# A host-side second layout of x for the pre-norm, and GpSimd powers for the inverse roots

## The chip, the cores and the metric

The kernel runs on one core of one Trainium2 chip. The metric is the device time of one launch in microseconds, the median of several runs. All other times here come from one profiled execution of the kernel before, whose trace lists every instruction of the five engines (TensorE, VectorE, ScalarE, GpSimd and SyncE, which issues the DMAs; in the profile PE, DVE, ACT, POOL and SP) and every DMA.

## What is computed

One layer of a hybrid decoder, 4096 tokens of 1024 channels, batch 1:

```python
shift, scale, gate = jnp.split(c_act @ ada_w + ada_b, 3, axis=-1)
h = _rmsnorm(x, g_pre) * (1.0 + scale[:, None]) + shift[:, None]
proj = h @ w_in                      # heads of three mixers and their gates
attn = _sliding_window_attention(aq, ak, av, sinks) * jax.nn.silu(ag)
rwkv = _rwkv7_mixer(h, rr, rk, rv, ...) * jax.nn.silu(rg)
gla = _gla_mixer(h, gq, gkk, gv, ...) * jax.nn.silu(gg)
y = jnp.concatenate([attn, rwkv, gla], axis=-1) @ w_out
return x + gate[:, None] * _rmsnorm(y, g_post)
```

Four places need an inverse root: the RMS norm of `x` (one number per token), the norm of the GLA output (per token and head), the group norm of the RWKV output (per position and head) and the RMS norm of `y` (per token). All products of h are done as three float16 products of high and low halves.

## The kernel before

**Two phases.** The tokens go in 16 blocks of 256. A first phase makes h of every block, writes it to memory (`hscr`) and runs the RWKV and GLA mixers, whose states pass from block to block. The second phase reads h back, does the attention, the gates, the output projection (seven products by a scheme of sums of halves) and the final norm. Ahead of the first block stands a prologue, which loads 8 MB of `ada_w` and works out the shift and scale columns `sh` and `gs` that the modulated norm needs.

**Streams and a planner.** Each phase is written as generators (`stage_a`, `stage_p`, `stage_q2`, ...), one per part and block. `emit` interleaves them; `Order` notes every instruction and `pin` then simulates the whole phase with a table of costs per instruction and fixes the order of the instructions on each engine. At run time each engine (and the SP queue, through which all the DMAs of this part go) works strictly in that order: an instruction that waits holds up everything behind it on its engine. Since all calls pass through one helper (`Lane`), almost every row of the profile has the line L334; rows are told apart by their tiles.

**Making h: `stage_a` (L1013).** For block i it loads 256 tokens into `xt`, with tokens on partitions (two groups of 128 tokens, 1024 channels each; one buffer), squares both groups on ScalarE with a running sum (`ssx`), turns the sums into inverse roots `rsx` on VectorE, scales both groups by them, and then needs channels on partitions. That takes 16 transposes of 128x128 on TensorE into a PSUM bank (tag `tr`, tile `tp`), four at a time; ScalarE moves each quarter out with scale and shift (`hf`), rounds it to float16 (`hT`), and VectorE takes the difference as the low half. `stage_p` (L1053) then multiplies `hT` with the weights (`pv`, `lp`, `zz`, `gqk`).

**Inverse roots.** `rsqrt(y, v, n)` (L428) makes `v**-0.5` for n columns on VectorE: a shift and an integer subtraction from the constant `magic`, then three Newton steps of three instructions, 11 dependent instructions in all. It is called in `stage_a` (`rsx`, n = 2), `gla_norm` (`orr`, n = 8), `stage_q2` (`yr`, n = 8) and `norm` in the second phase (`ry`, n = 1, twice per block). The last block's two groups use `last_norm` (L1878), which writes a similar sequence out (`ln`, nine instructions from the sum to the factor).

Of the kernel before, what the change touches and what calls it, by code (L numbers as in the profile page):

```python
# [63 lines left out]
class Order:  # L64
# [34 lines left out]
    def note(self, eng, name, outs, ins, func, r):  # L99
# [9 lines left out]
        if e == "PE":  # L109
            f32, lhs = ins[0].dtype == F32, self.region(ins[0])  # L110
            n = math.prod(o.shape[1:])
            _, p0, p1, _ = self.region(o)
            rows, cs = (lhs[1] // 32, (lhs[2] + 31) // 32), (p0 // 32, (p1 + 31) // 32)
            rows, cs = [(0, 4) if b - a > 2 else (a, b) for a, b in (rows, cs)]
            mode = (rows[1] - rows[0], cs[1] - cs[0])
            took = n * (2 if f32 else 1) / 2400 + 0.003
            took = max(took, 0.056 if not f32 else 0.0 if mode[1] < 4 else 0.109 if n > 16 else 0.21)
            issue = 0.017 if f32 and mode == (1, 2) else 0.009 if f32 and mode[0] == 1 else 0.007
            cells = [4 * a + b for a in range(*rows) for b in range(*cs)]
            st.array = (mode, cells, 2 if f32 and name == "matmul" else 1, took, issue)  # L120
            st.occ = st.lat = 0.0
        elif e == "SP":
            st.bytes = math.prod(ins[0].shape) * SIZE[ins[0].dtype]
            kb = st.bytes / 1024
            st.occ = 0.47
            st.lat = next((t for k, t in ((8, 1.9), (32, 2.0), (128, 2.3), (256, 2.6), (512, 3.5)) if kb <= k), 4.8)
        elif e == "Activation":
            st.occ = (0.05 if on_psum else 0.093) + 0.093 * (len(ins) - 1) + 0.832e-3 * n
            st.lat = st.occ + 0.1
            if len(outs) > 1:  # L130
                st.occ += 0.187
                st.lat = st.occ + 0.02
# [263 lines left out]


@with_exitstack
def hybrid_kernel(ctx, tc, x, rows, ada1, adaw, w1, wl, w2, wo, cst, abias, out):
    nc = tc.nc  # L400
    model = Model(tc)
    V = Lane(model, nc.vector, *LANES[0])
# [19 lines left out]
        a, b = VC[name]  # L422
        return vt[:, a:b] if j is None else vt[:, a + j : a + j + 1]

    magic = cp.tile([P, 16], I32, name="magic")
    V.memset(magic, 0x5F3759DF)

    def rsqrt(y, v, n):  # L428
        ii = st.tile([P, 16], I32, tag="nwi", name="nwi")
        tt = st.tile([P, 16], F32, tag="nwt", name="nwt")  # L430
# [213 lines left out]
    with ExitStack() as p1:  # L644

        soon = ("tables", "scolb", "uw", "w0p0", "w0p1", "one16", "mu_s", "mu_c", "a0h")
        late = ("td", "tf0", "tf1", "Sst0", "Sst1", "lnx")
        tags = ("gvh", "gvl", "hf", "b1", "gl", "bl", "cs", "ch", "gw", "zs", "gaw", "gacc", "zl0", "zl1", "zl2", "early",
                "zb1", "ta", "em", "ep", "zb0", "b2", "zb2", "kg", "kt", "egm", "egp", "qg", "vg", "c2", "middle",
                "AS", "osb", "c3", "KB", "ATm", "c1", "RA", "UV", "BK", "cd", "em0", "bon", "ysb", "rs", "Ss", "lasts")  # L650
        wk1 = {n: pool_of(p1, f"work1{n}", 1) for n in tags}
# [52 lines left out]
                SP.dma_start(t, cst[:, at : at + t.shape[-1]])  # L704
                at += t.shape[-1]

        def load_x(i):
            xt = t_x()
            SP.dma_start(xt, x[i * NT : (i + 1) * NT, :].rearrange("(a p) d -> p a d", p=P))
            E[i]["xt"] = xt  # L710


        scolb = pp.tile([P, KD, 32], F32, name="scolb")
# [299 lines left out]
        def stage_a(i):  # L1013

            yield [("a", i - 1), ("p", i - 2)]
            e = E[i]
            if i > 0:
                load_x(i)
            xt = e["xt"]
            yield [xt, "tr"]  # L1020
            xs = [xt[:, a, :] for a in range(2)]
            jx = wt([P, 2, NT], "hf", 2).rearrange("p a n -> p (a n)").bitcast(F16)
# [12 lines left out]
            e["hT"] = hT  # L1035
            for kp in range(KD // 2):

                tag = "tr" if i else ("tr", "y", "sq", "tr")[kp]
                tp = pst(tag, "tp").rearrange("p (a n) -> p a n", a=2)
# [4 lines left out]
                hf = wt([P, 2, NT], "hf", 2)  # L1044
                for kk in range(2):
                    k = 2 * kp + kk
                    S.activation(hf[:, kk, :], tp[:, kk, :], AF.Identity, scale=gs[:, k : k + 1], bias=sh[:, k : k + 1])
                S.activation(hT[:, 0, 2 * kp : 2 * kp + 2, :], hf, AF.Identity)
                V.tensor_sub(hT[:, 1, 2 * kp : 2 * kp + 2, :], hf, hT[:, 0, 2 * kp : 2 * kp + 2, :])
                yield [hf, "tr"] if i else None  # L1050
            SP.dma_start(hscr[i], hT.rearrange("p a k t -> p (a k t)"))

        def stage_p(i):  # L1053
# [823 lines left out]

    def last_norm(f, h, sums, xt):  # L1878

        v, y, t = [st.tile([P, 1], F32, tag=f"ln{n}", name=f"ln{n}") for n in range(3)]  # L1880
# [302 lines left out]
def _layout(inp):  # L2183
# [14 lines left out]
    def blk(w):  # L2198
# [25 lines left out]
    arrs = [("x", g["x"][0]), ("rows", rows), ("ada1", ada1), ("adaw", adaw), ("w1", w1), ("wl", wl), ("w2", w2),  # L2224
            ("wo", wob), ("cst", cst), ("abias", abt)]
    return {"in_" + n: np.ascontiguousarray(a) for n, a in arrs}

# [13 lines left out]
```

## Time and profile before

| | |
|---|---|
| median of 3 runs | 2062.37 us (2061.8 to 2066.6) |
| profiled execution, span of its instructions | 2056.7 us (the page has no other time of that execution) |
| instructions | 61151 |
| ScalarE busy | 1130.8 us (55%) |
| GpSimd busy | 220.5 us (11%) |
| DMA, mean over the span | 118 GB/s, 35.6% of the 16 engines on the main queue |
| first phase | the first block's values (`pv`) start at 40.1 us, the last inverse root of an RWKV output (`yr`) is done at 1072.3 us |
| second phase | from there to the end |

A row of a group of instructions reads: line, engine, operation, output<-inputs by the program's names, shapes, count, then busy time and mean length of one, then the idle time of the engine ahead of them and who ended it. TensorE's records overlap, because one matrix product is issued before the one ahead has ended: what a product costs the stream of TensorE is the distance from its start to the next start, not its length.

### The profile page before, as it was taken

The numbers are of one execution on the slowest core, as the hardware profiler recorded it, in microseconds if no ns is written. First come the engines' busy times: TensorE is split into PE (matmuls) and PEld (weight loads), VectorE is DVE, ScalarE is ACT, GpSimd is POOL, SyncE is SP. The second block draws the span as 40 slices with busy tenths as digits, with TensorE's granted clock in tenths as the row PEclk, the third lists the DMA queues.
The fourth block names the chain that finished last, engine by engine and source line by source line (L and its number), as shares of the span: only waits on it lengthen the run. The fifth ranks groups of instructions, "written<-read, shape, count | busy, mean of one in ns | idle before, by whom it ended". The sixth has DMA issues, their size and how long they took to land.

```text
span 2056.7 us, 61151 instructions
## 1 busy us (share of the span) xinstructions
PE 1950.2 (95%) x25123; PEld 1517.8 (74%) x25123; DVE 1590.3 (77%) x5120; ACT 1130.8 (55%) x2609; POOL 220.5 (11%) x405
## 2 busy tenths in 40 slices
PE   6899999999999999999898999999999999999997
PEld 3778787778787778887677677777787777777783
DVE  5877877787778986777667887887777877778877
ACT  5867666667767765664334544444444443444543
POOL 1511112321111121111100000000000000000000
PEclk9999999999999999999999999999999999999999
DMA  9433331433413332113433433433334343334314
GB/s 377 139 106 106 106 94 39 145 124 100 142 61 109 124 93 70 60 53 102 134 109 126 153 112 129 127 127 113 110 115 145 115 130 104 119 121 142 111 46 175
DMA packets 151714, 242.06 MB, mean 118 GB/s; under 512 B 48514, under 2 KB 100226, under 8 KB 147204
## 3 DMA queue, kind: packets, MB, share of 16 engines
q1 hardware_dynamic: 151284, 237.56, 35.6%
q8 instruction: 199, 3.26, 0.7%
q14 instruction: 87, 0.71, 0.1%
q10 hardware_dynamic: 144, 0.52, 0.1%
HBM read 177.20 MB, written 60.82 MB: 116 GB/s over the span
## 4 chain that ended last, share of the span: by engine, by line
PE 62%; DVE 21%; ACT 6%; DMA 6%; issue 3%; SPq 2%; DVEq 0%; POOL 0%; ACTq 0%; POOLq 0%
PE gp L334 16%; PE op L334 12%; PE zz L334 6%; PE qp L334 3%; PE lp L334 3%; PE pv L334 3%; PE kp L334 2%; PE gqk L334 2%; PE sc L334 2%; DVE mtp L334 2%; DVE q L334 2%; PE ovp L334 2%; DVE pr L334 2%; SPq L334 2%; DMA xt<-in_x 1%
## 5 line engine op out<-in xcount | busy, mean ns | idle before, releaser
L334 PEld LDWEIGHTS <-mtp 128*128 128x128 f16 x1344 | 130.4, 98 | 141.8 <-issue 4.6
L334 PE MATMUL op<-o,mtp 128*128 128x512 f16 x768 | 172.3, 379 | 0.1
L334 ACT ACTIVATE pr<-pr,nm,lsc 128x256 f32<-128x256 f32 (+1 forms) x256 | 149.2, 585 | 30.9 <-DVE nm L334 30.8
L334 PE MATMUL op<-ov,mtp 128*128 128x512 f16 x576 | 143.1, 379 | 1.3 <-DMA ov<-woscr 0.8
L334 PEld LDWEIGHTS <-hT 128*128 128x128 f16 x1536 | 118.9, 100 | 26.7 <-DVE kg L334 5.3
L334 DVE CUSTOM_DVE_ANT_0 pr<-sc,ab,kept 128x256 f32<-128x256 f32 (+1 forms) x256 | 108.5, 476 | 10.9 <-PE sc L334 10.2
L334 PE MATMUL pv<-gvh,hT 128*128 128x272 f16 x512 | 102.2, 291 | 6.4 <-DVE kg L334 4.5
L334 DVE TENSOR_TENSOR yv<-op,yv 128x512 f32<-128x512 f32 x105 | 70.4, 682 | 47.8 <-PE op L334 33.6
L334 ACT ACTIVATE ag<-gp,gh 128x512 f32<-128x512 f32 x64 | 43.7, 682 | 111.7 <-PE gp L334 111.7
L334 POOL COPY kT<-kT 128x512 f16<-128x512 f16 x15 | 10.2, 682 | 862.0 <-DVE kT L334 862.0
L334 PE MATMUL gqk<-hT,gqkh 128*128 128x256 f16 x512 | 90.3, 276 | 6.0 <-issue 4.2
L334 ACT ACTIVATE mtp<-yv,oi 128x1024 f16<-128x1024 f32 x30 | 34.3, 1144 | 111.8 <-DVE yv L334 111.3
L334 PE MATMUL qp<-hT,q1h 128*128 128x256 f16 x512 | 87.7, 276 | 5.9 <-DVE kT L334 5.9
L334 PE MATMUL lp<-hT,Lh 128*128 128x256 f16 x512 | 92.9, 276 | 0.2 <-ACT vg L334 0.2
L334 PE MATMUL zz<-hT,kh 128*128 128x256 f16 x512 | 92.3, 274 | 0.0
L334 PE MATMUL zz<-hT,vh 128*128 128x256 f16 x512 | 89.1, 275 | 3.4 <-DVE zb L334 3.4
L334 DVE SCALAR_TENSOR_TENSOR ag<-ag,gp 128x512 f32<-128x512 f32 x64 | 43.8, 684 | 62.4 <-ACT ag L334 62.3
L334 PE MATMUL zz<-hT,rh 128*128 128x256 f16 x512 | 91.8, 279 | 0.0
L334 PE MATMUL gp<-hT,q5h 128*128 128x256 f16 x512 | 87.6, 273 | 0.0
L334 PE MATMUL gp<-hT,q3h 128*128 128x256 f16 x512 | 85.5, 273 | 2.0 <-DVE yv L334 1.4
L334 PE MATMUL qp<-hT,q0h 128*128 128x256 f16 x512 | 85.2, 273 | 0.0
L334 PE MATMUL gp<-hT,q4h 128*128 128x256 f16 x512 | 84.9, 273 | 0.0
(460 smaller groups left out, 5981.7 us busy)
## 6 DMA issues: line engine op xcount, KB each, us to landing
ov<-woscr SPq DMA_DIRECT2D x96, 512.0 KB, 4.4
xt<-in_x SPq DMA_DIRECT2D x16, 1024.0 KB, 5.4
hscr<-hT SPq DMA_DIRECT2D x16, 1024.0 KB, 5.0
hT<-hscr SPq DMA_DIRECT2D x16, 1024.0 KB, 4.8
x<-in_x SPq DMA_DIRECT2D x30, 512.0 KB, 4.2
out<-yv SPq DMA_DIRECT2D x30, 512.0 KB, 2.9
cs<-in_w SPq DMA_DIRECT2D x56, 256.0 KB, 3.5
v<-vscr SPq DMA_DIRECT2D x128, 64.0 KB, 3.7
```

The costliest lines, as they stand in the source:

```text
L334: r = f(*args, **kw)
```

## The change

Three edits.

1. **x comes in twice.** The host also lays x out with channels on partitions (`xc`: block, 128 channels, 8 groups of channels, 256 tokens). `stage_a` loads the tokens in two halves into `xh` (512 KB each, one buffer, squared in place) only for the sums, and the block's `xc` (1 MB) into `xt`. The 16 transposes of x go. Instead the two columns of `rsx`, each spread by a broadcast over 128 columns, are transposed, so that a bank `rb` holds the factor of each of the 256 tokens in every partition; VectorE multiplies `xt` by it in two instructions of 1024 columns, and ScalarE's scale and shift now read `xt` in SBUF and write it in place.
2. **Inverse roots are one GpSimd instruction,** a power with exponent -0.5 from a constant tile, in all four callers and in `last_norm` (there with a multiplication by `oi` behind it).
3. **The planner** gets a cost for small GpSimd instructions (8 columns or fewer): 0.33 + 0.165 per column.

```diff
+            elif n <= 8:
+                st.occ = 0.33 + 0.165 * n
...
-    magic = cp.tile([P, 16], I32, name="magic")
-    V.memset(magic, 0x5F3759DF)
+    expo = cp.tile([P, 8], F32, name="expo")
+    V.memset(expo, -0.5)
     def rsqrt(y, v, n):
-        V.tensor_single_scalar(ii[:, :n], v.bitcast(I32), 1, op=ALU.logical_shift_right)
-        V.tensor_tensor(y.bitcast(I32), magic[:, :n], ii[:, :n], op=ALU.subtract)
-        for _ in range(3):
-            V.tensor_mul(tt[:, :n], y, y)
-            V.scalar_tensor_tensor(tt[:, :n], tt[:, :n], -0.5, v, op0=ALU.mult, op1=ALU.mult)
-            V.scalar_tensor_tensor(y, tt[:, :n], 1.5, y, op0=ALU.add, op1=ALU.mult)
+        G.tensor_tensor(y, v, expo[:, :n], op=ALU.pow)
...
-        load_x(0)
+        load_tokens(0, 0)
+        load_channels(0)
...
+        def load_tokens(i, a):
+            xh = wt([P, D], "xh", 1)
+            SP.dma_start(xh, x[i * NT + a * P : i * NT + (a + 1) * P, :])
+            E[i]["xh"] = xh
+        def load_channels(i):
+            xt = E[i]["xt"] = t_x().rearrange("p a d -> p (a d)").rearrange("p (k t) -> p k t", k=KD)
+            SP.dma_start(xt, xc[i])
...
-            if i > 0:
-                load_x(i)
-            xt = e["xt"]
-            yield [xt, "tr"]
-            xs = [xt[:, a, :] for a in range(2)]
             for a in range(2):
-                S.activation(jx, xs[a], AF.Square, accum_out=ssx[:, a : a + 1])
-                yield [ssx]
+                if i or a:
+                    load_tokens(i, a)
+                yield [e["xh"]]
+                S.activation(e["xh"], e["xh"], AF.Square, accum_out=ssx[:, a : a + 1])
+            if i:
+                load_channels(i)
...
             rsqrt(rsx, msx, 2)
+            yield [rsx, xt, "tr"]
+            rb = pst("tr", "rb")[:, :NT]
             for a in range(2):
-                V.tensor_scalar(xs[a], xs[a], rsx[:, a : a + 1], None, op0=ALU.mult)
-                yield [xt, "tr"]
+                PE.transpose(rb[:, a * P : (a + 1) * P], rsx[:, a : a + 1].to_broadcast([P, P]), ident)
+            for h in range(2):
+                ks = slice(4 * h, 4 * h + 4)
+                V.tensor_tensor(xt[:, ks], xt[:, ks], rb.rearrange("p (o t) -> p o t", o=1).to_broadcast([P, 4, NT]), op=ALU.mult)
             for kp in range(KD // 2):
-                for kk in range(2):
-                    for a in range(2):
-                        k = 2 * kp + kk
-                        PE.transpose(tp[:, kk, a * P : (a + 1) * P], xs[a][:, k * P : (k + 1) * P], ident)
...
-                    S.activation(hf[:, kk, :], tp[:, kk, :], AF.Identity, scale=gs[:, k : k + 1], bias=sh[:, k : k + 1])
+                    S.activation(xt[:, k], xt[:, k], AF.Identity, scale=gs[:, k : k + 1], bias=sh[:, k : k + 1])
...
     def last_norm(f, h, sums, xt):
         V.scalar_tensor_tensor(v, sums[:, 0:1], 1e-6, sums[:, 1:2], op0=ALU.add, op1=ALU.add)
-        V.tensor_single_scalar(t.bitcast(I32), v.bitcast(I32), 1, op=ALU.logical_shift_right)
-        V.tensor_tensor(y.bitcast(I32), magic[:, 0:1], t.bitcast(I32), op=ALU.subtract)
-        for c in (3.0, 12.0, 768.0):
-            V.scalar_tensor_tensor(t, y, y, v, op0=ALU.mult, op1=ALU.mult)
-            V.scalar_tensor_tensor(y, t, -c, y, op0=ALU.add, op1=ALU.mult)
-        V.scalar_tensor_tensor(y, y, -1.0 / 8192, f["oi"], op0=ALU.mult, op1=ALU.mult)
+        rsqrt(y, v, 1)
+        V.tensor_mul(y, y, f["oi"])
...
+    xc = g["x"][0].reshape(NS, NT, KD, P).transpose(0, 3, 2, 1)
```

**How the order moves: TensorE, in the middle of the first phase.** Of the kernel before, while one block's `lp` is multiplied (`Lh`, `Ll` are weights, `hT` the block's h; `up`, `gap` belong to the mixers), with the next block's transposes `tp` in between:

```order
L334 LDWEIGHTS Ll
L334 MATMUL lp<-hT,Ll 128x256
L334 MATMUL tp<-first,xt 128x128 x2
L334 MATMUL gap<-qb,kg 64x256 x4
L334 MATMUL up<-rs,tf_524 64x64 x4
L334 MATMUL tp<-first,xt 128x128 x2
L334 LDWEIGHTS Lh
```

Of the changed kernel, at the like place:

```order
L336 MATMUL yp<-Sst_502,RA 64x64
L336 MATMUL gp<-kept,zlT 64x128 x4
L336 MATMUL rb<-first,rsx 128x128 x2
L336 LDWEIGHTS Lh
L336 MATMUL lp<-hT,Lh 128x256
```

What were four such groups of four per block is one pair `rb`; the weights and products around them stay.

**VectorE, the end of one block's RWKV output.** Of the kernel before (`ve` is the variance, `ysb` the output; the `p2e`, `tsc` and `TT` rows between are other streams' work):

```order
L334 TENSOR_SCALAR ve<-mv 128x8
L334 TENSOR_TENSOR ysb<-ysb,mv 128x512
L334 TENSOR_SCALAR nwi<-ve 128x8
L334 TENSOR_SCALAR p2e<-wtot 128x1
L334 TENSOR_TENSOR tsc<-TT,AS 128x8x10
L334 TENSOR_TENSOR yr<-magic,nwi 128x8
L334 TENSOR_SCALAR p2e<-p2e 128x1
L334 TENSOR_REDUCE TT<-tsc 128x8
L334 TENSOR_TENSOR nwt<-yr 128x8
```

Of the changed kernel, up to the instruction that waits for GpSimd's `yr` (`zb`, `ta`, `RA` are other streams' work):

```order
L336 TENSOR_SCALAR ve<-mv 128x8
L336 TENSOR_TENSOR ysb<-ysb,mv 128x512
L336 SCALAR_TENSOR_TENSOR zb_8106<-zz,mu_c,zs 128x256
L336 SCALAR_TENSOR_TENSOR ta<-ta,rn 128x512
L336 TENSOR_TENSOR RA<-zb_7932,ep 128x8x64
L336 TENSOR_TENSOR ysb<-ysb,yr 128x512
```

The 11 small instructions have left VectorE, and the multiplication by `yr` stands four rows behind `ve`.

**SP, the prologue's loads.** Of the kernel before, from the first block's x to its second loads:

```order
L334 DMA xt<-in_x 128x2x1024
L334 DMA aw<-in_ada 128x1024 x8
L334 DMA stgRA<-in_ada 128x1024
L334 DMA stg<-in_ada 128x1024 x4
L334 DMA stgRA<-in_ada 128x1024
L334 DMA stgUV<-in_ada 128x1024
L334 DMA stgKB<-in_ada 128x1024
L334 DMA tables<-in_cst 128x771
L334 DMA masks<-in_cst 128x416
L334 DMA kept<-in_cst 128x392
L334 DMA stgRA<-in_w 128x1024
```

Of the changed kernel, the two ends of the same stretch:

```order
L336 DMA xh<-in_x 128x1024
L336 DMA xt<-in_xc 128x2048
L336 DMA aw<-in_ada 128x1024 x8
L336 DMA stgRA<-in_ada 128x1024
L336 DMA stg<-in_ada 128x1024 x4
```

```order
L336 DMA kept<-in_cst 128x392
L336 DMA xh<-in_x 128x1024
L336 DMA stgRA<-in_w 128x1024
```

Half a megabyte more stands ahead of the `ada_w` loads, and the second half of the first block's tokens comes only behind them, with the next weights behind it.

More of the change, by code (lines that the diff above doesn't have):

```diff
@@ L398, in hybrid_kernel @@
 @with_exitstack
-def hybrid_kernel(ctx, tc, x, rows, ada1, adaw, w1, wl, w2, wo, cst, abias, out):
+def hybrid_kernel(ctx, tc, x, xc, rows, ada1, adaw, w1, wl, w2, wo, cst, abias, out):
     nc = tc.nc
@@ L647, in hybrid_kernel @@
         late = ("td", "tf0", "tf1", "Sst0", "Sst1", "lnx")
-        tags = ("gvh", "gvl", "hf", "b1", "gl", "bl", "cs", "ch", "gw", "zs", "gaw", "gacc", "zl0", "zl1", "zl2", "early",
+        tags = ("gvh", "gvl", "xh", "b1", "gl", "bl", "cs", "ch", "gw", "zs", "gaw", "gacc", "zl0", "zl1", "zl2", "early",
                 "zb1", "ta", "em", "ep", "zb0", "b2", "zb2", "kg", "kt", "egm", "egp", "qg", "vg", "c2", "middle",
@@ L705, in load_constants @@
                 at += t.shape[-1]
[L707 to L710, printed above, removed]
+        def load_tokens(i, a):
[5 more added lines that the diff above has]
+            SP.dma_start(xt, xc[i])
         scolb = pp.tile([P, KD, 32], F32, name="scolb")
@@ L1016, in stage_a @@
             e = E[i]
-            if i > 0:
-                load_x(i)
-            xt = e["xt"]
-            yield [xt, "tr"]
-            xs = [xt[:, a, :] for a in range(2)]
-            jx = wt([P, 2, NT], "hf", 2).rearrange("p a n -> p (a n)").bitcast(F16)
             ssx = st.tile([P, 2], F32, tag="ssx", name="ssx")
             for a in range(2):
-                S.activation(jx, xs[a], AF.Square, accum_out=ssx[:, a : a + 1])
-                yield [ssx]
+                if i or a:
[4 more added lines that the diff above has]
+                load_channels(i)
+            xt = e["xt"]
+            yield [ssx]
             msx = st.tile([P, 2], F32, tag="msx", name="msx")
@@ L1030, in stage_a @@
             rsqrt(rsx, msx, 2)
+            yield [rsx, xt, "tr"]
+            rb = pst("tr", "rb")[:, :NT]
             for a in range(2):
-                V.tensor_scalar(xs[a], xs[a], rsx[:, a : a + 1], None, op0=ALU.mult)
-                yield [xt, "tr"]
+                PE.transpose(rb[:, a * P : (a + 1) * P], rsx[:, a : a + 1].to_broadcast([P, P]), ident)
             hT = t_hT()
             e["hT"] = hT
+            for h in range(2):
+                ks = slice(4 * h, 4 * h + 4)
+                V.tensor_tensor(xt[:, ks], xt[:, ks], rb.rearrange("p (o t) -> p o t", o=1).to_broadcast([P, 4, NT]), op=ALU.mult)
             for kp in range(KD // 2):
-                tag = "tr" if i else ("tr", "y", "sq", "tr")[kp]
-                tp = pst(tag, "tp").rearrange("p (a n) -> p a n", a=2)
-                for kk in range(2):
-                    for a in range(2):
-                        k = 2 * kp + kk
-                        PE.transpose(tp[:, kk, a * P : (a + 1) * P], xs[a][:, k * P : (k + 1) * P], ident)
-                hf = wt([P, 2, NT], "hf", 2)
-                for kk in range(2):
-                    k = 2 * kp + kk
-                    S.activation(hf[:, kk, :], tp[:, kk, :], AF.Identity, scale=gs[:, k : k + 1], bias=sh[:, k : k + 1])
-                S.activation(hT[:, 0, 2 * kp : 2 * kp + 2, :], hf, AF.Identity)
-                V.tensor_sub(hT[:, 1, 2 * kp : 2 * kp + 2, :], hf, hT[:, 0, 2 * kp : 2 * kp + 2, :])
-                yield [hf, "tr"] if i else None
+                ks = slice(2 * kp, 2 * kp + 2)
+                for k in (2 * kp, 2 * kp + 1):
+                    S.activation(xt[:, k], xt[:, k], AF.Identity, scale=gs[:, k : k + 1], bias=sh[:, k : k + 1])
+                S.activation(hT[:, 0, ks], xt[:, ks], AF.Identity)
+                V.tensor_sub(hT[:, 1, ks], xt[:, ks], hT[:, 0, ks])
+                yield [xt]
             SP.dma_start(hscr[i], hT.rearrange("p a k t -> p (a k t)"))
@@ L1878, in last_norm @@
     def last_norm(f, h, sums, xt):
-        v, y, t = [st.tile([P, 1], F32, tag=f"ln{n}", name=f"ln{n}") for n in range(3)]
+        v, y = [st.tile([P, 1], F32, tag=f"ln{n}", name=f"ln{n}") for n in range(2)]
         V.scalar_tensor_tensor(v, sums[:, 0:1], 1e-6, sums[:, 1:2], op0=ALU.add, op1=ALU.add)
-        V.tensor_single_scalar(t.bitcast(I32), v.bitcast(I32), 1, op=ALU.logical_shift_right)
-        V.tensor_tensor(y.bitcast(I32), magic[:, 0:1], t.bitcast(I32), op=ALU.subtract)
-        for c in (3.0, 12.0, 768.0):
-            V.scalar_tensor_tensor(t, y, y, v, op0=ALU.mult, op1=ALU.mult)
-            V.scalar_tensor_tensor(y, t, -c, y, op0=ALU.add, op1=ALU.mult)
-        V.scalar_tensor_tensor(y, y, -1.0 / 8192, f["oi"], op0=ALU.mult, op1=ALU.mult)
+        rsqrt(y, v, 1)
+        V.tensor_mul(y, y, f["oi"])
         z, r0 = f["end"][h], (NS - 1) * NT + h * P
@@ L2223, in _layout @@
                           masks, bd, gk2, sinks], axis=1)
-    arrs = [("x", g["x"][0]), ("rows", rows), ("ada1", ada1), ("adaw", adaw), ("w1", w1), ("wl", wl), ("w2", w2),
+    xc = g["x"][0].reshape(NS, NT, KD, P).transpose(0, 3, 2, 1)
+    arrs = [("x", g["x"][0]), ("xc", np.ascontiguousarray(xc)), ("rows", rows), ("ada1", ada1), ("adaw", adaw), ("w1", w1), ("wl", wl), ("w2", w2),
             ("wo", wob), ("cst", cst), ("abias", abt)]
```

2 lines of the change are left out of this document (removed).

## The prediction

> **What bounds the kernel now.** I read the page's span and busy times first, then a view that cuts the span into stretches, because the two phases have different limits.
>
> ```profile
> span 2056.7 us, 61151 instructions
> PE 1950.2 (95%) x25123; PEld 1517.8 (74%) x25123; DVE 1590.3 (77%) x5120; ACT 1130.8 (55%) x2609; POOL 220.5 (11%) x405
> core 0: us, PE busy (x) PEld busy (x) DVE busy (x) ACT busy (x) POOL busy (x), PEclk, DMA share, GB/s
> 0.00:41.00 41.00, 22.30 (x98) 8.37 (x99) 23.35 (x117) 19.31 (x36) 2.37 (x17) 0.92 0.97 379
> 153.00:875.00 722.00, 694.79 (x11103) 565.69 (x11102) 577.79 (x2123) 490.42 (x1074) 140.89 (x262) 0.99 0.32 98
> 1075.00:2033.00 958.00, 937.27 (x9700) 709.59 (x9698) 749.19 (x2073) 436.49 (x1105) 9.62 (x14) 1.00 0.38 121
> 2033.00:2057.00 24.00, 9.97 (x46) 4.24 (x44) 15.54 (x37) 3.86 (x9) 2.49 (x2) 0.82 0.44 163
> ```
>
> The prologue (to 41 us) is bound by DMA, at a share of 0.97. After it TensorE is busy 96% of the first phase's middle (694.79 of 722) and 98% of the second phase (937.27 of 958), at a granted clock of 0.99 to 1.00. VectorE is at 80% and 78%, ScalarE at 68% and 46%. So an instruction counts where it leaves TensorE's stream, or where it makes TensorE wait. The view of waits, from 100 to 1000 us, says which waits exist:
>
> ```profile
> PE pv L334 <- DVE kg L334: 4.5, 3, 2.2
> ACT hf L334 <- PE tp L334: 17.6, 19, 2.4
> ```
>
> Columns: who waits for whom, us in all, times, longest. TensorE's wait on VectorE here is small (4.5 us); ScalarE's 17.6 us for the transposes are on an engine with slack.
>
> **The transposes.** This is the main term. Their record is longer than what they cost the stream, so I take the distance from one start to the next:
>
> ```profile
> L334 PE MATMUL tp<-first,xt x256: 272/273/475, 20.0 to 896.4; 128*128 128x128 f32 x128
> 666.39 0.60 PE L334 MATMUL tp<-first,xt 128*128 128x128 f32 x4
> 666.83 0.38 PE L334 MATMUL zz<-hT,rh 128*128 128x256 f16 x2
> 840.14 0.55 PE L334 MATMUL tp<-first,xt 128*128 128x128 f32 x3
> 840.52 0.27 PE L334 MATMUL zz<-hT,kh 128*128 128x256 f16 x1
> ```
>
> Four in 0.44 us give 0.109 us each, three in 0.38 give 0.127. Over the 240 of blocks 1 to 15 I added up all such distances: 30.3 us, 0.126 each. A block has 16 now and two `rb` then, so 14 go: 14 x 0.126 x 15 blocks = **26.5 us** (22.9 at 0.109). Taking `rb` at the price of a `tp` is an estimate, since it too is a 128x128 f32 transpose. The Trainium skill, "TensorE: Matmul & The Clock Gate", Part 4, puts a transpose at about 275 ns; the record's 273 agrees in length, but the starts 0.109 apart show the records overlapping, and by 275 the same count would come to 58 us.
>
> **VectorE and ScalarE.** The rows of the inverse roots and of what takes the place of the scaling:
>
> ```profile
> L334 DVE SCALAR_TENSOR_TENSOR yr<-nwt,yr x48: 151/159/270, 184.1 to 1072.3; 128x8 f32<-128x8 f32 x48
> L334 DVE TENSOR_TENSOR nwt<-ry x90: 149/159/163, 1146.5 to 2032.8; 128x1 f32<-128x1 f32 x90
> L334 DVE TENSOR_SCALAR xt<-xt,rsx 128x1024 f32<-128x1024 f32 x32 | 23.2, 747 | 0.6
> L334 DVE TENSOR_TENSOR bon<-bp,zb 128x256 f32<-128x256 f32 x32 | 12.0, 416 | 9.6 <-PE bp L334 9.6
> L334 DVE TENSOR_TENSOR yv<-op,yv 128x512 f32<-128x512 f32 x105 | 70.4, 682 | 47.8 <-PE op L334 33.6 <-issue 13.9
> L334 ACT ACTIVATE hf<-tp,sh,gs 128x256 f32<-128x256 f32 x128 | 65.9, 559 | 18.1 <-PE tp L334 17.6 <-DVE sh L334 0.2
> L334 ACT ACTIVATE k<-ta,kam,kah 128x256 f32<-128x256 f32 x32 | 17.6, 593 | 1.2 <-DVE rs L334 1.2
> ```
>
> Three inverse roots per first-phase block are 33 instructions of about 0.16, 5.3 us of VectorE. The two new products read PSUM at 1024 columns: from 256 columns (416 ns) to 512 (682) it is 266 per 256, so 682 + 2 x 266 = 1214 ns each, against 747 now: +0.94 per block. Net relief about 4.4 us per block, 70 us over 16 blocks, and 22 x 0.16 = 3.5 us per block in the second phase. ScalarE's `hf` from SBUF goes from 559 to 593 at most, +0.27 per block, and its wait of 17.6 goes. Since these engines are not what the stream waits for, I count all this as nothing in the likeliest case, and as a gain in rival A. In the second phase nothing leaves TensorE: 0.
>
> **The GpSimd powers.** No power stands in this trace. The nearest rows:
>
> ```profile
> L334 POOL COPY bl<-bl 128x1 f32<-128x1 f32 x15 | 4.0, 268 | 0.7
> L334 POOL TENSOR_TENSOR gacc<-gaw 128x128 f32<-128x128 f32 x16 | 10.7, 669 | 0.7
> L334 POOL TENSOR_TENSOR qb<-qg,kept 128x512 f32<-128x512 f32 x32 | 39.1, 1243 | 55.4 <-DVE qg L334 55.3
> ```
>
> Bounds: 0.27 us (one column, one input) and 1.24 us (two inputs, 512 columns). I take 0.67, the two-input row nearest in width. A power may well be dearer per element than a product; rival C goes past the upper bound for that. It replaces a chain that I read here:
>
> ```profile
> 17.38 0.16 DVE L334 TENSOR_TENSOR nwt<-rsx 128x2 f32<-128x2 f32 x1
> 17.57 0.16 DVE L334 SCALAR_TENSOR_TENSOR nwt<-nwt,msx 128x2 f32<-128x2 f32 x1
> ```
>
> Starts 0.19 apart, 11 of them: 2.1 us. So at 0.67, and even at 1.24, the result comes sooner than now. The change adds a wait: `ysb*yr` on VectorE now waits for GpSimd, and in VectorE's order these stand between `ve` and it:
>
> ```profile
> L334 DVE TENSOR_TENSOR ysb<-ysb,mv 128x512 f32<-128x512 f32 x16 | 11.0, 685 | 0.0
> L334 DVE SCALAR_TENSOR_TENSOR zb<-zz,mu_c,zs 128x256 f32<-128x256 f32 x96 | 44.0, 477 | 9.0 <-ACT zs L334 8.8
> L334 DVE SCALAR_TENSOR_TENSOR ta<-ta,rn 128x512 f32<-128x512 f32 x16 | 11.9, 747 | 0.0
> L334 DVE TENSOR_TENSOR RA<-zb,ep 128x512 f32<-128x512 f32 x16 | 11.9, 747 | 0.0
> ```
>
> 0.685 + 0.477 + 0.747 + 0.747 = 2.66 us of cover, in most blocks (the last block has only the first row). A power up to 2.66 us is hidden; beyond it VectorE stands, and the next `zb`, `ta` and the mixers' PSUM copies stand behind it, for which TensorE waits. The second phase's `ry` has about 0.8 us of cover for one group and none for the other; what waits is the end of a finished block, so 0.
>
> **Loads.** A block's x is 1 MB in one load now, and 2 MB in three loads then, two of which share one buffer and so come in series with their squares.
>
> ```profile
> SPq L334 <- PE tp L334: 75.5, 8, 26.0
> xt<-in_x SPq DMA_DIRECT2D x16, 1024.0 KB, 5.4
> ```
>
> That load already holds SP for up to 26 us until the transposes free `xt`; then the last differences of `hT` free it, later by ScalarE's and VectorE's part of a block. The weights, `hscr` and `wo` pieces of other parts are queued behind on SP. The added 16 MB over some 1030 us are 16 GB/s, and the windows show the DMA at a share of 0.32 with 98 GB/s, so room for it; the loads run a block ahead of use, so I take 0. Without that lead a late load costs its 5.4 us per block, 81 us, of which B takes a small share.
>
> **Prologue and tail.** Both have small terms of their own.
>
> ```profile
> 30.78 1.05 PE L334 MATMUL adp<-stgUV,scolb 128*32 128x512 f32 x4 [0.22 <-DMA stgUV<-in_ada]
> 32.08 1.05 PE L334 MATMUL adp<-stgKB,scolb 128*32 128x512 f32 x4 [0.25 <-DMA stgKB<-in_ada]
> 38.08 1.47 ACT L334 ACTIVATE hf<-tp,sh,gs 128x256 f32<-128x256 f32 x3 [0.18 <-DVE sh L334]
> ```
>
> One 512 KB load shifts what follows by 32.08 - 30.78 = 1.30 us. Half a megabyte stands newly ahead of `ada_w`, +1.3, and the block's second half of tokens lands after the constants, with the weights another 1.3 later: up to 2.6, and a chain of square, power, `rb` and two products behind a late load could make it 4. In the other direction, block 0 no longer waits for transposes on their way through PSUM. I take **+2**, with ends 0.6 and 4.
>
> ```profile
> 2045.46 0.15 DVE L334 SCALAR_TENSOR_TENSOR ln<-lsum 128x1 f32<-128x1 f32 x1
> 2046.04 3.23 DVE L334 SCALAR_TENSOR_TENSOR ln<-ln,ln 128x1 f32<-128x1 f32 x6
> 2046.77 2.49 POOL L334 TENSOR_TENSOR pr<-pr,xo 128x512 f32<-128x512 f32 x2 [139.79 <-ACT pr L334]
> ```
>
> At the end, six `ln` steps take 3.23 us while GpSimd adds `pr`; one alone takes 0.15. The chain from 2045.46 to 2049.3 becomes one power and a product, but that power stands behind the two additions on GpSimd, which end at 2046.77 + 2.49 = 2049.26. From -2.5 to +1, I take **-0.8**: some steps go, and the wait for GpSimd stays.
>
> The same rows show a rule against this change. The Trainium skill, "SBUF — State Buffer", section "Who interferes with whom", says that a VectorE instruction with two SBUF inputs contends with a GpSimd instruction that reads SBUF; the trace agrees (3.23 us against 6 x 0.15). By it the cover above shrinks, and 48 powers at 0.67 would hold VectorE 32 us of its 70 us of relief, which leaves the forecast as it is.
>
> **The sum.** 2056.7 - 26.5 + 2 - 0.8 = 2031.4 us of span. The page gives no other time of that execution; the median of the runs, 2062.4, lies 5.7 above its span, so about **2037 us**, 1.2% less.
>
> **Rivals.** *A, more:* VectorE's 70 us of relief and the freed PSUM bank also shorten TensorE's waits. For: TensorE is idle 3.8% of the first phase (27.2 of 722) but 2.2% of the second (20.7 of 958). Falling to 2.2% over some 1000 us gives 16 us more: about 2021. Against: the rows name few waits on VectorE.
>
> *B, partly hidden:* the transposes fill holes between dependent products of the mixers. In TensorE's order 143 of 256 have such a product right before or behind them; if only the other 113 are worth anything, 26.5 x 113/256 = 11.7: 2056.7 - 11.7 + 2 - 0.8 + 5.7 = 2052. Against: the 240 distances near 0.109 to 0.127 look like a full stream. Loads late on SP, now three in series per block, would give the same sort of time.
>
> *C, slower:* VectorE stands in its order for GpSimd's power. Two of 8 columns per block, 32 in all, each losing its length beyond 2.66 us. It eats the forecast's 25.3 us at 2.66 + 25.3/32 = 3.45 us. At 5 us, 32 x 2.34 = 75 us, 2037 + 75 = 2112. For: the trace has no price of a power, and GpSimd takes 669 ns for a product of 128 columns. Against: GpSimd would need 0.4 us per column.
>
> *D, not on the path:* TensorE's stream is bound by the mixers' chain from block to block and keeps its time: -0.8 + 2, so about 2063.
>
> **Chances and range.** Forecast (2028 to 2046: the low price 0.109, the ends of prologue and tail) 0.50; A 0.23; B 0.13; C 0.09; D 0.05. A run can tell about 0.3%, 6.2 us, from no change: faster means below 2056.2, slower above 2068.6. Faster holds the forecast, A and most of B: 0.83; same takes D and the edge of B: 0.08; slower is C: 0.09. The range from 2016 to 2058 leaves out C, a stronger A and D.
>
> **What would show it.** Right: in the first phase `rb` x32 in place of `tp` x256, the distance of blocks falling by about 1.8 us, TensorE's busy share unchanged; the second phase's length within 1 us of before. Powers under 2.66 us, and no wait of `ysb` on GpSimd. First `hf` 2 us later than 38.08. A is right if the block distance falls by 2.8 us or more and TensorE's idle share with it; B if it falls by about 0.8 and idle time grows; C if `ysb` or `osb` waits for GpSimd's `yr` or `orr` appear with microseconds each. It would be wrong if SP's three loads make squares late, so that h itself becomes late and `pv` waits for `hT`.

## The result and the profile after

The changed kernel takes 2023.35 us, the median of 4 runs (2021.1 to 2025.2), against 2062.09 for the kernel before: a ratio of 0.9824, with a 95% interval of 0.9808 to 0.9839. That is 38.7 us less. The prediction had 25 us less (2037) and a range of 2016 to 2058.

The page of the changed kernel, its span and its busy times:

```profile
span 2022.1 us, 59931 instructions
PE 1919.5 (95%) x24899; PEld 1483.7 (73%) x24899; DVE 1506.7 (75%) x4246; ACT 1130.1 (56%) x2609; POOL 311.3 (15%) x485
```

TensorE has 224 products fewer (25123 to 24899), VectorE 874 instructions fewer, GpSimd is busy 91 us longer. To place the 34.6 us between the spans I use two marks, the first product of the values (`pv`, block 0) and the first and last product of the output in the rows `op<-o` (the rows `op<-ov` begin 4.9 us sooner and end 2.6 us later in both kernels). Before:

```profile
L334 PE MATMUL pv<-gvh,hT x512: 276/279/434, 40.1 to 937.5; 128*128 128x272 f16 x171
L334 PE MATMUL op<-o,mtp x768: 376/379/379, 1128.6 to 2040.8; 128*128 128x512 f16 x192
```

After:

```profile
L336 PE MATMUL pv<-gvh,hT x512: 276/279/434, 43.6 to 910.0; 128*128 128x272 f16 x171
L336 PE MATMUL op<-o,mtp x768: 376/379/634, 1091.7 to 2008.1; 128*128 128x512 f16 x192
```

| stretch | before | after | difference |
|---|---|---|---|
| prologue, to the first `pv` | 40.1 | 43.6 | +3.5 |
| first phase, to the first `op` | 1088.5 | 1048.1 | **-40.4** |
| second phase, to the last `op` | 912.2 | 916.4 | +4.2 |
| tail, to the end of the span | 15.9 | 14.0 | -1.9 |

The whole gain is in the first phase. The view by stretches (length, then the busy time of TensorE, its weight loads, VectorE, ScalarE and GpSimd, then the granted clock and the DMA share) from the second block to the end of that phase, before:

```profile
93.00:1123.00 1030.00, 978.09 (x15356) 796.02 (x15355) 795.69 (x2884) 648.57 (x1437) 178.60 (x336) 0.98 0.32 101
```

and after, with the stretch that the prediction used:

```profile
153.00:875.00 722.00, 697.17 (x11464) 563.24 (x11464) 575.68 (x1761) 512.87 (x1122) 197.91 (x311) 0.99 0.38 117
96.00:1086.00 990.00, 947.87 (x15150) 766.23 (x15150) 764.66 (x2377) 648.00 (x1435) 246.21 (x383) 0.99 0.38 120
```

TensorE's busy time falls by 30 us and its idle time from 51.9 (1030 - 978.09) to 42.1. So there are two gains here: work that left, and idle time that left. Over the whole span, by the two pages, 30.7 of the 34.6 us are busy time (1950.2 to 1919.5) and 3.9 are idle time.

The new instructions, of the changed kernel (shortest, median and longest in ns, then first and last start):

```profile
L336 PE MATMUL rb<-first,rsx x32: 272/273/474, 39.5 to 852.1; 128*128 128x128 f32 x32
L336 DVE TENSOR_TENSOR xt<-xt,rb x32: 1175/1210/1222, 40.2 to 853.9; 128x1024 f32<-128x1024 f32 x32
L336 POOL TENSOR_TENSOR ry<-sy,expo x30: 539/544/1518, 1109.3 to 1991.1; 128x1 f32<-128x1 f32 x30
L336 POOL TENSOR_TENSOR rsx<-msx,expo x16: 692/697/755, 38.7 to 668.2; 128x2 f32<-128x2 f32 x16
L336 POOL TENSOR_TENSOR orr<-og,expo x16: 1632/1638/2091, 130.6 to 996.9; 128x8 f32<-128x8 f32 x16
L336 POOL TENSOR_TENSOR yr<-ve,expo x16: 1632/2007/2305, 193.2 to 1035.3; 128x8 f32<-128x8 f32 x16
```

The products by `rb` take 1210 ns (estimated 1214). A power takes 544 ns for one column, 697 for two, 1638 for eight: 153 to 157 ns for each further column. For eight that is above both bounds that the nearest rows gave. VectorE's waits for the two 8-column powers are small all the same (us in all, times, longest):

```profile
DVE ysb L336 <- POOL yr L336: 2.4, 5, 1.5
DVE osb L336 <- POOL orr L336: 0.2, 1, 0.2
```

In the second phase the longer 4.2 us hold a wait of TensorE for weights read back from memory, 0.8 us before and 3.5 after (at the row's end):

```profile
L334 PE MATMUL op<-ov,mtp 128*128 128x512 f16 x576 | 143.1, 379 | 1.3 <-DMA ov<-woscr 0.8 <-DVE q L334 0.5
```

```profile
L336 PE MATMUL op<-ov,mtp 128*128 128x512 f16 x576 | 144.0, 381 | 3.6 <-DMA ov<-woscr 3.5
```

That wait can't be all of it: the kernel before under a second plan (below) has 2.6 us of it and a second phase of 911.9 us. Among all profiled kernels here, the ten whose `ry` is a GpSimd power have second phases of 913.5 to 916.4 us by the same marks, the four with `ry` on VectorE 910.2 to 912.2. So the longer phase goes with the powers; `ry` alone was not moved back.

### The profile page after: what moved, and what is told of

It reads as the page before. It is cut to its first block, busy times and chain, and to the rows that moved or that the text cites. A ratio compares the mean times of both kernels' runs of the same rounds, so it can differ in the third digit from the quotient of the medians.

```text
span 2022.1 us, 59931 instructions
## 1 busy us (share of the span) xinstructions
PE 1919.5 (95%) x24899; PEld 1483.7 (73%) x24899; DVE 1506.7 (75%) x4246; ACT 1130.1 (56%) x2609; POOL 311.3 (15%) x485
## 4 chain that ended last, share of the span: by engine, by line
PE 54%; DVE 22%; ACT 9%; DMA 8%; issue 4%; SPq 2%; POOL 1%; DVEq 0%; ACTq 0%; POOLq 0%
PE gp L336 16%; PE op L336 12%; PE zz L336 4%; PE qp L336 3%; PE pv L336 2%; PE lp L336 2%; PE kp L336 2%; PE sc L336 2%; DVE pr L336 2%; PE ovp L336 2%; DVE q L336 2%; DVE mtp L336 2%; SPq L336 2%; DMA cs<-in_wo 1%; DVE tsc L336 1%
## 5 line engine op out<-in xcount | busy, mean ns | idle before, releaser
L336 ACT ACTIVATE mtp<-yv,oi 128x1024 f16<-128x1024 f32 x30 | 34.5, 1149 | 155.1 <-DVE yv L336 114.4
L336 POOL TENSOR_TENSOR ry<-sy,expo 128x1 f32<-128x1 f32 x30 | 19.1, 638 | 588.3 <-DVE sy L336 588.3
L336 PE MATMUL gp<-hT,q6h 128*128 128x256 f16 x512 | 85.2, 273 | 0.0
```

Of the source, the lines that this page charges most:

```text
L336: r = f(*args, **kw)
```

## The experiments

All kernels were timed in 5 rounds against the kernel before, whose median in those rounds was 2057.7 to 2060.5. By those medians the change's 38.7 us, taken in other rounds, are 34 to 37.

### One part of the change at a time

The second layout alone: the changed kernel with the 11 instructions on VectorE in all callers, `last_norm` as before.

```diff
-        G.tensor_tensor(y, v, expo[:, :n], op=ALU.pow)
+        V.tensor_single_scalar(ii[:, :n], v.bitcast(I32), 1, op=ALU.logical_shift_right)
+        V.tensor_tensor(y.bitcast(I32), magic[:, :n], ii[:, :n], op=ALU.subtract)
+        for _ in range(3):
...
```

> The changed kernel with the inverse roots left on VectorE in all callers (the second layout of x stays). Theory 1: the transposes that left are worth 26.5 us by their distances, and the other 14 us of the first phase come from VectorE's relief; then this kernel loses the 14 us again and ends near 2037. Theory 2: the whole 40 us of the first phase come from the transposes and what stood around them (their PSUM bank, the order), and VectorE's small instructions were hidden; then it stays near 2023.

Measured: **2072.35** (2070.3 to 2074.2), ratio 1.0054 (1.0040 to 1.0068). It is slower than the kernel before, which neither theory had. The powers alone, on the kernel before:

```diff
-        V.tensor_single_scalar(ii[:, :n], v.bitcast(I32), 1, op=ALU.logical_shift_right)
...
+        G.tensor_tensor(y, v, expo[:, :n], op=ALU.pow)
```

> The kernel before with the GpSimd powers alone (and the planner's cost for them); x is transposed as before. Theory 1 (VectorE's relief is worth 14 us): near 2048. Theory 2 (the relief is hidden): 2060 to 2064. If VectorE stood for the powers: above 2068.

Measured: **2050.28** (2045.9 to 2052.5), ratio 0.9947 (0.9933 to 0.9960). One part costs 12 us, the other saves 10, and both together save 37 by the same median. The same stretch of 980 us, all of it in the first phase, in four kernels; before:

```profile
100.00:1080.00 980.00, 933.72 (x14872) 758.36 (x14870) 757.89 (x2793) 622.05 (x1369) 173.00 (x331) 0.99 0.32 100
```

second layout alone:

```profile
100.00:1080.00 980.00, 915.56 (x14600) 734.87 (x14600) 773.11 (x2752) 612.01 (x1359) 169.51 (x335) 0.97 0.36 113
```

and one row of the view of waits (us, times, longest), of the kernel before, of the second layout alone and of both parts:

```profile
PE yt L334 <- DVE ysb L334: 3.3, 4, 1.4
PE yt L336 <- DVE ysb L336: 11.8, 8, 3.0
PE yt L336 <- DVE ysb L336: 5.9, 5, 3.1
```

powers alone:

```profile
100.00:1080.00 980.00, 937.48 (x14944) 759.12 (x14943) 709.92 (x2303) 628.83 (x1392) 238.69 (x379) 0.99 0.33 103
```

both (the change):

```profile
100.00:1080.00 980.00, 938.09 (x15079) 758.03 (x15078) 754.79 (x2356) 642.52 (x1423) 243.93 (x380) 0.99 0.38 121
```

Read VectorE's column (the third) against TensorE's (the first). With the layout alone VectorE is the busiest of the four (773) and TensorE the idlest (64 us of 980, clock 0.97), and TensorE waits for `ysb` on VectorE 11.8 us. With the powers alone VectorE has slack (710), and TensorE, with its transposes, is what is left. That reads as two limits, so that lowering one alone runs into the other. It is a reading: the stretch holds a different share of the work in each kernel, so its columns alone don't prove it. The run with VectorE's work added back, below, tests it.

### The price of the transposes

The changed kernel with 16 transposes into `rb` per block instead of 2:

```diff
-            for a in range(2):
+            for n in range(16):
+                a = n % 2
                 PE.transpose(rb[:, a * P : (a + 1) * P], rsx[:, a : a + 1].to_broadcast([P, P]), ident)
```

> The changed kernel with the two transposes of a block made 16, all into the same bank, the last two counting; nothing else is added. It prices 14 transposes per block alone: at 0.126 us each 14 x 16 x 0.126 = 28 us, near 2051. If a transpose costs its record's 0.273 us: 61 us, near 2084. If transposes of that number fall into holes of the stream: below 2035.

Measured: **2048.94** (2043.9 to 2050.3), 25.6 us over the changed kernel: 25.6/224 = 0.114 us each, between the 0.109 and 0.127 that the starts gave and far from the record's 0.273. The ranges of the runs of both kernels allow 0.083 to 0.130. It ends where the powers alone end (2050), as it should if that kernel differs from the changed one in its transposes.

### Is the cover of the powers real?

Three powers in a row where one stood, for the 8-column roots, with the same total cost in the planner:

```diff
+        if n == 8:
+            w = st.tile([P, 8], F32, tag="pw", name="pw")
+            for _ in range(2):
+                G.tensor_tensor(w, v, expo, op=ALU.pow)
         G.tensor_tensor(y, v, expo[:, :n], op=ALU.pow)
...
-                st.occ = 0.33 + 0.165 * n
+                st.occ = (0.33 + 0.165 * n) / (3 if n == 8 else 1)
```

> The changed kernel with three powers in a row on GpSimd wherever 8 columns are raised (two go to a tile that nobody reads), with the planner told a third of the cost for each, so that the order stays. One such power took 1.64 us, so the result comes after 4.9 us, past the 2.66 us of cover in VectorE's order. If VectorE stands for the rest and that reaches TensorE in full: 32 x 2.26 = 72 us, near 2095. If half of it does: near 2059. If the cover is in truth longer, or TensorE runs on: below 2030.

Measured: **2140.01** (2132.5 to 2143.9), ratio 1.0373 (1.0357 to 1.0389): 117 us over the changed kernel, more than the worst case expected. VectorE's waits for the powers in it, up to 1150 us:

```profile
DVE ysb L336 <- POOL yr L336: 46.6, 14, 4.6
DVE osb L336 <- POOL orr L336: 41.2, 16, 3.3
```

The last of the three powers, among the rows of `yr`:

```profile
L336 POOL TENSOR_TENSOR yr<-ve,expo x16: 1630/1637/1638, 203.8 to 1155.1; 128x8 f32<-128x8 f32 x16
```

And the stretch of 980 us:

```profile
100.00:1080.00 980.00, 874.74 (x13605) 693.56 (x13604) 685.82 (x2107) 598.89 (x1301) 326.05 (x424) 0.95 0.36 110
```

The first of the three takes about 2.0 us in most blocks and the other two 1.64 each, so the result comes after about 5.3 us. A wait for `yr` is 46.6/14 = 3.3 us, so about 2 us are covered, not 2.66, and one power of 2 us just fits. (The planned order did not stay as intended everywhere: in more than half of the blocks other rows stand between `ve` and its reader than in the changed kernel.) VectorE's 93 us of waits (the two rows and 4.9 us behind 1150) became 117 us of time. TensorE's idle time in this stretch is 105 us and its clock 0.95, so part of the excess is a lower clock; the table in the next section has its size.

The third edit, the planner's cost, taken away (it then takes such a power for 0.43 us):

```diff
-            elif n <= 8:
-                st.occ = 0.33 + 0.165 * n
```

> The changed kernel without its third edit: the planner takes a power of 8 columns for 0.43 us, where the trace has 1.64, and places its reader accordingly early. If the plan needs the true cost, VectorE waits up to 1.2 us at each of 32 readers: up to 39 us, between 2030 and 2062. If the readers stand late anyway: 2020 to 2028.

Measured: **2045.84** (2039.1 to 2048.5), 22.5 us over the changed kernel. Its readers stand too early, and every one of the 32 waits:

```profile
DVE ysb L334 <- POOL yr L334: 19.0, 16, 1.4
DVE osb L334 <- POOL orr L334: 16.6, 16, 1.5
```

That is 35.6 us against 2.6: the cover is made by the planner, which needs the true cost for it.

### Occupied time or the chain?

What costs 49 us between the layout alone (2072) and both parts (2023): the time that the small instructions hold VectorE, or their late results? The changed kernel with the 11 instructions added back, on results that nobody reads:

```diff
         G.tensor_tensor(y, v, expo[:, :n], op=ALU.pow)
+        y = st.tile([P, 8], F32, tag="nwy", name="nwy")[:, :n]
+        V.tensor_single_scalar(ii[:, :n], v.bitcast(I32), 1, op=ALU.logical_shift_right)
...
```

> The changed kernel as it is, with the 11 small VectorE instructions of every inverse root added back into a tile that nobody reads (the powers still give the results). It has VectorE's load of the kernel with the second layout alone (2072), but not its chain of results. If VectorE's occupied time is what the first phase cannot bear beside fewer products on TensorE: 2060 to 2072. If the chain (a result 11 instructions late) was the cost there: 2023 to 2035.

Measured: **2053.80** (9 runs, a wide 2045.5 to 2059.7), between the two expectations: VectorE's added work, on results that nobody reads, costs about 30 of the 49 us. (This kernel is planned anew too, so a part of the 30 can be its order.) Its stretch of 980 us:

```profile
100.00:1080.00 980.00, 931.16 (x14784) 749.70 (x14782) 779.13 (x2821) 632.20 (x1397) 237.95 (x380) 0.98 0.38 119
```

Then the two kinds of roots apart, x's on VectorE:

```diff
+        if n == 2:
+            V.tensor_single_scalar(ii[:, :n], v.bitcast(I32), 1, op=ALU.logical_shift_right)
...
+            return
         G.tensor_tensor(y, v, expo[:, :n], op=ALU.pow)
```

> The changed kernel with the roots of x's norms alone (2 columns, one per block) on VectorE. That is 11 of the 33 small instructions of a block, 28 us of VectorE's 85, but it is the one root whose result goes on through TensorE (rb) to the block's h. If occupied time counts: a third of the 49 us between 2023 and 2072, near 2039. If x's own chain counts: 2055 or more. If neither: 2023.

Measured: **2042.68** (2040.7 to 2048.0), near the share of a third. And the 8-column roots on VectorE (the same edit with `n == 8`):

> The changed kernel with the 8-column roots (orr and yr) alone on VectorE, 22 of the 33 small instructions of a first-phase block. If occupied time counts: two thirds of 49 us, near 2055. If x's own chain counts: 2030 or less. These two powers take 1.64 us and two VectorE waits come with them, which go here: a few us less than the proportion.

Measured: **2080.19** (2079.3 to 2080.4), above both expectations and above the kernel with all roots on VectorE (2072). The two add up to 19 + 57 = 76 us, not 49, so the parts don't add, and each kernel has an order of its own.

```profile
100.00:1080.00 980.00, 911.69 (x14459) 728.73 (x14458) 745.30 (x2588) 617.89 (x1357) 184.36 (x347) 0.97 0.36 112
```

VectorE is busy for 745 us there, less than in the changed kernel (755), and yet TensorE is idle for 68. So VectorE's occupied time alone does not say what holds the phase.

The pages show what TensorE loses in these kernels. All have the same 24899 products:

| kernel | span | TensorE busy | TensorE idle | granted clock |
|---|---|---|---|---|
| both parts (the change) | 2022.1 | 1919.5 | 102.6 | 0.989 |
| x's roots on VectorE | 2039.1 | 1923.4 | 115.7 | 0.987 |
| planner's cost taken away | 2043.6 | 1921.8 | 121.8 | 0.988 |
| idle results added | 2047.3 | 1932.9 | 114.4 | 0.980 |
| second layout alone | 2070.1 | 1936.7 | 133.4 | 0.978 |
| 8-column roots on VectorE | 2078.5 | 1942.6 | 135.9 | 0.977 |
| three powers in a row | 2142.2 | 1961.5 | 180.7 | 0.968 |

A loss has two parts, more idle time and the same products taking longer at a lower clock. The second part is 17 of 48 us with the layout alone, 13 of 25 with idle results, 23 of 56 with the 8-column roots and 42 of 120 with three powers. The loss of clock times the changed kernel's busy time would give 21, 17, 23 and 40 (an estimate), so the clock is of the right size to account for it. Which of VectorE's rows start the idle time, and why the clock is lower, stays open: of TensorE's waits, those on `ysb` and `osb` are 5.9 us in the kernel with the 8-column roots on VectorE.

### Is it one lucky order?

The planner's fixed cost of a VectorE instruction is changed in three kernels, which moves rows and nothing else:

```diff
-            fixed, rate = 0.065 + 0.06 * (cols > 0), 1.04e-3
+            fixed, rate = 0.075 + 0.06 * (cols > 0), 1.04e-3
```

The kernel before:

> The kernel before under a second plan: the planner's fixed cost of a VectorE instruction is 0.075 us where it was 0.065, which changes the order it pins and no instruction. It and the next two say how much of the differences is the luck of one order. If order luck is below 5 us: 2055 to 2065. If it is of the size of the differences found (10 to 50 us): anything outside that.

Measured: **2047.01** (2044.3 to 2054.0), ratio 0.9946 (0.9927 to 0.9964). The second layout alone:

> The changed kernel with the roots on VectorE (2072 before), under the second plan. If VectorE's small instructions hold the phase once the transposes are gone: 2062 to 2080, no gain over the kernel before under the same plan. If the loss was one bad order: near 2037, the forecast without VectorE's relief.

Measured: **2068.16** (2065.6 to 2074.6). Its stretch again shows the idle TensorE and the lower clock:

```profile
100.00:1080.00 980.00, 911.48 (x14521) 731.84 (x14519) 768.62 (x2748) 615.14 (x1359) 168.12 (x335) 0.97 0.36 113
```

Both parts:

> The changed kernel under the second plan. If its gain does not hang on one order: 2018 to 2030. If it was a good order by luck: 2035 or more.

Measured: **2024.42** (2019.7 to 2028.5).

| | roots on VectorE | roots on GpSimd |
|---|---|---|
| x transposed | 2062.1, second plan 2047.0 | 2050.3 |
| second layout | 2072.4, second plan 2068.2 | 2023.4, second plan 2024.4 |

An order can be worth 11 us: the kernel before had one that is 11 us worse than another (the two fixed costs are the only plans tried, and the second plan's runs lie in two groups, near 2046 and near 2054), and the change measured against the better one saves 22.6 us, not 38.7. The lower row moves by 4 and 1 us only. So two statements hold under both plans: the layout alone doesn't gain, and with it the roots on GpSimd are worth 44 to 49 us. The 10 us of the powers alone are no larger than what an order does.

### The prologue

Block 0 alone is made by transposes of x as before, the other 15 as in the change:

```diff
-        load_tokens(0, 0)
-        load_channels(0)
+        E[0]["x0"] = t_x()
+        SP.dma_start(E[0]["x0"], x[0:NT, :].rearrange("(a p) d -> p a d", p=P))
...
+            if i == 0:
+                yield from stage_a0()
+                return
```

> The changed kernel, with block 0 alone made from x by 16 transposes as in the kernel before, so that the prologue loads 1 MB of x ahead of the adaptation weights and no second layout. If the prologue's 3.5 us are its loads and the longer chain to the first h: first products back near 40 us and 2020. If the order of the phase gives it back: 2023.

Measured: **2019.97** (2018.3 to 2022.6), ratio 0.9817 (0.9804 to 0.9830), the fastest kernel of this study. Its first product is back:

```profile
L336 PE MATMUL pv<-gvh,hT x512: 276/279/434, 40.4 to 905.2; 128*128 128x272 f16 x171
```

43.6 to 40.4 us at the start, and 3.4 us in the medians: the prologue's price was the second layout of block 0, on a stretch that is bound by DMA and in which TensorE has room for 16 transposes. The two medians lie 3.4 us apart with runs that overlap (2021.1 to 2025.2 and 2018.3 to 2022.6), so the size is rough.

## Why the prediction was right, and what it had wrong

Direction and range held. The forecast itself missed by 13.7 us, and the terms account for that: -13.9 in the first phase, +1.5 in the prologue, +4.2 in the second phase, -1.1 in the tail, and -4.5 in the step from span to median.

**The transposes** were sized rightly: 26.5 us forecast, 25.6 measured by putting them back. But that price holds only where the roots have left VectorE. With VectorE as it was, their removal gave nothing (2072 against 2062, 2068 against 2047).

**VectorE's relief** is the mis-sized term. The step read "I count all this as nothing in the likeliest case", since VectorE was busy for 80% and few of TensorE's waits named it. With the second layout in place the relief is worth 44 to 49 us under both plans, and without it the 26.5 us are not gained at all. The forecast let them come by themselves; that the range held all the same is luck in this step, because both edits came together.

How much of the miss is relief is less sure. In the first phase 13.9 us came on top of the 26.5 forecast; in the stretches above, TensorE has 30.2 us less busy and 9.8 us less idle time. But 11 us are what another order of the kernel before is worth, and against that order the change gains 22.6 us, less than the 25 forecast. Rival A had 16 us for the relief and 2021 in all, at a chance of 0.23. Its reason was half right: idle time of TensorE did go (51.9 to 42.1 us in the phase), though its share in the stretch that A used fell from 3.8% only to 3.4%, not to 2.2%. The sign that was to tell the two apart doesn't: the distance of blocks, with 1.8 us less for the forecast and 2.8 for A, fell by 2.1 from one block's first `pv` to the next (59.2 to 57.1, the mean of 15) and by 3.1 from one `ysb<-ysb,mv` to the next (59.2 to 56.1).

The runs suggest why the small waits misled: with the roots on VectorE, TensorE's wait for `ysb` was 3.3 us beside the transposes and 11.8 without them. That VectorE's work costs time once they are gone is seen in the kernel with idle results, 30 us slower. That occupied time is the whole of it is not shown, and the 8-column roots on VectorE speak against it.

**The powers** were taken at 0.67 us with 1.24 as the upper bound; eight columns take 1.64, and 2.0 for most `yr`. "0.685 + 0.477 + 0.747 + 0.747 = 2.66 us of cover, in most blocks" added the lengths of records, where the starts count, as they did for the transposes. One of the sixteen blocks of the changed kernel has just these rows, and there they begin 2.21 us ahead of the reader (their lengths add up to 2.51), and the power begins 2.04 us ahead of it:

```profile
490.10 2.01 POOL L336 TENSOR_TENSOR yr<-ve,expo 128x8 f32<-128x8 f32 x1 [1.36 <-DVE ve L336]
489.93 0.68 DVE L336 TENSOR_TENSOR ysb<-ysb,mv 128x512 f32<-128x512 f32 x1
490.53 0.47 DVE L336 SCALAR_TENSOR_TENSOR zb<-zz,mu_c,zs 128x256 f32<-128x256 f32 x1
490.93 0.68 DVE L336 SCALAR_TENSOR_TENSOR ta<-ta,rn 128x512 f32<-128x512 f32 x1
491.52 0.68 DVE L336 TENSOR_TENSOR RA<-zb,ep 128x512 f32<-128x512 f32 x1
492.14 0.69 DVE L336 TENSOR_TENSOR ysb<-ysb,yr 128x512 f32<-128x512 f32 x1
```

In VectorE's order the other blocks have other rows there; the last has only the first one and the longest wait, 1.5 us. The two errors together left no margin where the forecast had 2 us. That little wait followed (2.4 and 0.2 us) is the planner's doing: its cost of 1.65 in the diff was the true price, and without it 22.5 us go. The prediction did not use that number for the power, though it stood in the diff. Rival C's point of 3.45 us rests on the same 2.66; with about 2 us of cover the forecast's gain would be gone at about 2 + 25.3/32 = 2.8 us (an estimate).

**Shared memory reads.** The prediction weighed the Trainium skill, "SBUF — State Buffer", section "Who interferes with whom", by which a VectorE instruction with two SBUF inputs contends with a GpSimd instruction that reads SBUF. The runs agree in kind: in the changed kernel the eleven `yr` that start within 0.15 us of the end of `ve`, beside `ysb<-ysb,mv`, take 1.94 to 2.31 us, and the five that start 0.6 us later or more take 1.63 to 1.70. Here it is the power that is longer, by about 0.37 us, and `ysb<-ysb,mv` is not (684 ns, 685 before). No run shows the 32 us that the prediction took from it as VectorE's loss.

**Prologue** +2 forecast, +3.5 measured, inside its ends of 0.6 and 4, with the mechanism as told. **Second phase:** 0 forecast, +4.2. That was wrong too: all ten kernels whose `ry` is a power have a longer second phase than the four without, by 1.3 us at the least. A weight load that TensorE waits 2.7 us longer for is in it; how the powers lead to it was not tried. **Tail:** -0.8 forecast, -1.9. The power of the last group stands behind the two additions on GpSimd, as foreseen:

```profile
2011.95 2.91 POOL L336 TENSOR_TENSOR pr<-pr,xo 128x512 f32<-128x512 f32 x2 [1.02 <-ACT pr L336]
2014.82 0.54 POOL L336 TENSOR_TENSOR ln<-ln,expo 128x1 f32<-128x1 f32 x1
```

**From span to median** I added 5.7 us, the distance of one profiled execution from the median of others. The changed kernel's profiled execution took 2023.94 us for a span of 2022.1, so what lies around the span is 1.8; the rest was the scatter of the kernel before (2057 to 2067).

## What to carry to other kernels

An engine that is busy for 77% can be the limit behind the one that is busy for 95%. Price a change by both: here relief of TensorE alone gave nothing and of VectorE alone 10 us, no more than an order does, while both together gave 22.6 to 38.7 us, and the waits on the second engine were small until the first was relieved. When work moves to another engine under a planned order, give the planner the true price of the moved instruction, since the cover is made by it. And before crediting a few parts in a thousand to an edit, plan the kernel before a second time: here another order alone was worth 11 us.

## What was not expected of the hardware

A GpSimd power costs about 0.39 us and 0.156 us per column (544, 697 and 1638 ns for 1, 2 and 8 columns of 128 partitions), where a sum of two inputs of 128 columns took 669 ns in the kernel before: eight columns of a power cost more than 512 columns of a product (1243). And the granted clock was mostly lower where TensorE lost more time in the stretch of 980 us: 0.99 with 42 us idle (the changed kernel), 0.97 with 64 (layout alone), 0.95 with 105 (three powers). But it was 0.98 with 49 us idle (idle results) and 0.99 with 61 (planner's cost taken away), so the sum of idle time alone does not set it.
